# Moving the split weights by 16 bytes in the on-chip memory of a two-layer decoder trunk

## The chip, the cores and the metric

The kernel runs on one core of a Trainium2 chip. The metric is the device time of one execution in microseconds (us). Lower is better. The kernel before took 2561.69 us (median of three runs, 2560.36 to 2563.14).

## What is computed

The reference is a decoder trunk of two layers over 256 tokens of width 2048, all in float32. Layer 0 mixes the tokens by retention (8 heads), layer 1 by a short gated convolution. A SwiGLU feed-forward network (FFN) of inner width 5632 follows in each. Every sub-layer normalizes its input, scales and shifts it by values made from a conditioning vector, and multiplies its output by a gate made from the same vector.

```python
for i in range(DEPTH):                      # 2 layers
    mod = (silu(c) @ w_mod[i] + b_mod[i])   # six vectors of 2048
    sh1, sc1, g1, sh2, sc2, g2 = split(mod, 6)
    h = rms_norm(x, norm1_g[i]) * (1 + sc1) + sh1
    x = x + g1 * mixer(h)                   # layer 0: retention, layer 1: short convolution
    h = rms_norm(x, norm2_g[i]) * (1 + sc2) + sh2
    a, b = split(h @ ffn_w_in[i], 2)
    x = x + g2 * ((silu(a) * b) @ ffn_w_out[i])
return rms_norm(x, final_g)
```

## The kernel before

Nearly all the work is products of weights with 256 tokens. TensorE runs them in the type float32r, which carries fewer bits than float32. So each operand is split into a high part (the value rounded to float32r) and a low part (the rest), and three of the four partial products are summed: high times high, high times low, low times high.

**The way of a weight.** The weights lie in device memory in the order of their use, in 456 blocks of 128 x 2048 floats (1 MB). `fetch` (L378) loads a block into one of four `raw` tiles from SyncE's queue. `prepare` (L393) takes half a block, 1024 columns: ScalarE rounds it into `hi` (L419), VectorE subtracts that from the half and writes `lo` (L422). The tiles `hi` and `lo` have five places each (`PLACES`) of 1024 columns, used in turn. `take` (L434) hands the next columns of the place in front to TensorE and lets `prepare` run ahead.

**How a place is read.** A matmul has a stationary operand, 128 columns that are loaded into the array ahead of it, and a moving operand that streams through. The places are read in two ways:

- As the stationary operand. In `product` (L462) the 128 weight columns stand still and the activations move: 512 columns with `hi` (L472, high and low part of the 256 tokens at once), then 256 columns with `lo` (L475). `packed` (L497) does the same for narrow groups in three matmuls of 256 columns (L534 to L536), and `normed` (L644) at the start of a sub-layer with 258, 256 and 258 columns (L667 to L669). These carry the mixers' projections, the first columns of each FFN's input, and the output products of all but the last FFN.
- As the moving operand. In `by_token` (L492) and `sevens` (L1201) the activations of 128 tokens stand still and 512 weight columns move, in the three matmuls of `thrice` (L482): `hi` (L485), `lo` (L486), `hi` again with the activations' low part (L487). These carry most of the FFNs' input, the last FFN's output, and the values and gates of the retention. `sevens` forms a 2 x 2 block product from seven products instead of eight. Its sums of activations lie in tiles of their own (`sums`, `in_cb`, `u`, `sum`, `low`, `sums_of_tokens`).

The rest of the work shares VectorE and ScalarE with the splitting: the modulation vectors (VectorE, L326 and, at the start, L798), activations, gates and norms. The order of TensorE's instructions is written out by hand; the other engines are scheduled from priorities.

**Where the tiles lie.** A tile's pool gives it a start in each partition's memory; starts are rounded up to 32 bytes, and the tiles of a pool lie in the order in which they are first asked for. In the program before, `hi` starts at byte 43,616, `lo` at 64,096, the four `raw` at 84,576, 92,768, 100,960 and 109,152, an empty tile `aside` of 32 bytes at 117,344, and `h_all`, the activations, at 117,376. In steps of 64 bytes `hi`, `lo` and `raw` thus start at 32, `h_all` at 0. A place is 4096 bytes long and columns are taken 128 or 512 at a time, so every weight operand starts at 32 of 64. `rows_at(o)` (L628) lays 16 rows of 2048 bytes into `h_all`, from its start on (0 of 64) or from 120 floats on (`EARLIER`, 480 bytes, 32 of 64). The retention and both FFNs use the second, the convolution and the first columns of outputs the first. `normed` reads 16 rows (`raw_all`) of 514 floats, so row k starts at 8k bytes, modulo 128. The empty tiles `beside_cb`, `aside`, `beside`, `apart` and `beside_sums` do nothing but shift what lies behind them.

Of the kernel before, what the change touches and what calls it, by code (L numbers as in the profile page):

```python
# [10 lines left out]
F32 = mybir.dt.float32  # L11
F32R = mybir.dt.float32r
# [5 lines left out]
P = 128  # L18
# [14 lines left out]
HALF = 1024  # L33
# [18 lines left out]
STEPS = (8, 8, 24)  # L52
RAW_BUFS = 4
PLACES = 5
FETCHED, PLAIN, WARM, ADDED = 2, 3, (5, 0, 0, 0, 0, 0, 0, 8), ()
SIDE_BY_SIDE, HELD_SIDE_BY_SIDE = (5, 6, 7), (1, 3)
LEFT, ENDS, EARLIER = 8, 2, 120
# [207 lines left out]
def trunk(ctx: ExitStack, tc: tile.TileContext, x_in, c_in, pos_in, w_mod, cols_in, gain_in, tab_in, w_all, out):  # L265
# [3 lines left out]
    wpool = ctx.enter_context(tc.tile_pool(name="wpool", bufs=1))  # L269
# [123 lines left out]
    def prepare(between=None):  # L393
# [17 lines left out]
        elif piece == 5:  # L411
            nc.vector.tensor_tensor(b[3], b[3], b[1], op=ALU.subtract)
            raw = b[3]
        width, at = raw.shape[1], HALF * (taken_places[0] % PLACES)
        taken_places[0] += -(-width // HALF)
# [7 lines left out]
        ready.extend((hi[:, o], lo[:, o], o.stop - o.start) for o in steps)  # L423

    taken_places = [0]
    split_weights = [
        wpool.tile([P, PLACES * HALF], F32R, tag=tag, name=tag) for tag in ("hi", "lo")
    ]
    prepared = [0]

    def fits():
        return prepared[0] < len(pieces) and len(ready) + 1 + (pieces[prepared[0]][1] == 6) <= PLACES

# [184 lines left out]
    hpool = ctx.enter_context(tc.tile_pool(name="hpool", bufs=1))  # L618
# [2 lines left out]

    hpool.tile([P, LEFT], F32, tag="aside", name="aside")
    h_all = hpool.tile([P, (KT + 1) * (ENDS + 2 * S)], F32R, tag="h", name="h")
    hpool.tile([P, 88], F32, tag="beside", name="beside")

# [931 lines left out]
```

## Time and profile before

| what | value |
|---|---|
| median of three runs | 2561.69 us (2560.36 to 2563.14) |
| the profiled execution: span from the first to the last instruction | 2558.4 us |
| the median beside that span | 3.3 us more |
| granted TensorE clock, mean | 0.998 of full speed |
| VectorE busy | 2354.7 us (92%) |
| ScalarE busy | 1351.2 us (53%) |
| moved by DMA | 689.47 MB |

The profile is one execution seen by the hardware profiler; for it no time is given but its span. PE is TensorE's matmuls, PEld its loads of stationary operands, DVE is VectorE, ACT is ScalarE, POOL is GpSimd, SP is SyncE. In a row of a group, `bank<-hi,h` names what is written and what is read, `x1540` is the count, and the numbers behind the bar are the busy time in us, the mean duration of one in ns, and the idle time ahead of them. A matmul's duration in the profile holds the way through the array and overlaps the next one; what a matmul costs in a stream is the distance from its start to the start of the next, which the timeline shows to 10 ns.

### The profile page before, as it was taken

What the parts mean: (1) busy time and instruction counts of PE and PEld (TensorE: products, weight loads), DVE (VectorE), ACT (ScalarE), POOL (GpSimd) and SP (SyncE); (2) the same over time, 40 slices, a digit from 0 to 9 for tenths busy, and PEclk for the clock granted to TensorE, in tenths of its full rate; (3) what the DMA queues carried; (4) which work ended last, traced back from release to release, by engine and by line L of the source; (5) the groups of instructions that cost most, each with busy time, mean ns of one, the idle gap of its engine ahead of it and who ended that gap; (6) DMA issues with size and microseconds to landing.
All of it is one profiled execution on the core that took longest, in us unless ns stands there. A gap on an engine that the chain in (4) does not pass through costs nothing.

```text
span 2558.4 us, 34761 instructions
## 1 busy us (share of the span) xinstructions
PE 2539.3 (99%) x13237; PEld 2181.4 (85%) x13237; DVE 2354.7 (92%) x2968; ACT 1351.2 (53%) x1799; POOL 179.3 (7%) x234
## 2 busy tenths in 40 slices
PE   8999999999999999999999999999999999999998
PEld 7898888888889888888888898888998888888886
DVE  7989999898899999889999899888989999999998
ACT  5544543454456554345555454445566555555554
POOL 0000121011110001000000012000000000000001
PEclk9999999999999999999999999999999999999999
DMA  9987888879875667866667879888846465555653
GB/s 399 396 329 264 319 317 340 333 287 331 325 281 213 237 234 293 336 249 228 216 228 299 328 270 344 314 306 309 323 158 215 180 230 214 181 214 183 228 183 146
DMA packets 96695, 689.47 MB, mean 269 GB/s; under 512 B 10744, under 2 KB 12168, under 8 KB 13456
## 3 DMA queue, kind: packets, MB, share of 16 engines
q1 hardware_dynamic: 96528, 687.25, 72.2%
q8 instruction: 103, 1.69, 0.3%
q14 instruction: 64, 0.52, 0.1%
HBM read 685.11 MB, written 2.11 MB: 269 GB/s over the span
## 4 chain that ended last, share of the span: by engine, by line
PE 94%; DVE 3%; DMA 1%; ACT 1%; issue 1%; POOL 0%; SPq 0%; ACTq 0%; POOLq 0%; DVEq 0%
PE bank L472 22%; PE bank L487 17%; PE bank L485 17%; PE bank L486 17%; PE bank L475 11%; DVE lo L422 1%; PE bank L667 1%; PE bank L669 1%; PE bank L668 1%; PE bank L536 1%; PE bank L535 1%; PE bank L534 1%; DVE raw L798 1%; DMA raw<-w_all 1%; PE bank L1290 1%; PE bank L1067 1%
## 5 line engine op out<-in xcount | busy, mean ns | idle before, releaser
L419 ACT CAST hi<-raw 128x1024 fp32r<-128x1024 f32 (+1 forms) x984 | 991.1, 1019 | 936.7 <-PE bank L487 325.1
L422 DVE TENSOR_TENSOR lo<-raw,hi 128x1024 fp32r<-128x1024 f32 (+1 forms) x984 | 1143.3, 1179 | 125.6 <-ACT hi L419 116.7
L485 PE MATMUL bank<-hi,h 128*128 128x512 f32 x1540 | 602.9, 391 | 0.0
L487 PE MATMUL bank<-hi,h 128*128 128x512 f32 x1540 | 601.2, 390 | 0.0
L486 PE MATMUL bank<-lo,h 128*128 128x512 f32 x1540 | 601.1, 390 | 0.0
L326 DVE SCALAR_TENSOR_TENSOR raw<-raw,cb 128x2048 f32<-128x2048 f32 x160 | 365.4, 2285 | 8.2 <-DMA raw<-w_mod 8.0
L472 PE MATMUL bank<-h,hi 128*128 128x512 f32 x1012 | 352.8, 392 | 0.0
L487 PEld LDWEIGHTS bank<-hi,h 128*128 128x128 f32 x1540 | 289.4, 188 | 61.0
L485 PEld LDWEIGHTS bank<-hi,h 128*128 128x128 f32 x1540 | 289.6, 188 | 58.1
L486 PEld LDWEIGHTS bank<-lo,h 128*128 128x128 f32 x1540 | 289.7, 188 | 57.5
L472 PE MATMUL bank<-mid,hi 128*128 128x512 f32 x920 | 319.4, 391 | 0.0
L475 PE MATMUL bank<-h,lo 128*128 128x256 f32 x1012 | 285.0, 282 | 0.0
L475 PE MATMUL bank<-mid,lo 128*128 128x256 f32 x920 | 259.7, 282 | 0.0
L472 PEld LDWEIGHTS bank<-h,hi 128*128 128x128 f32 x1012 | 190.1, 188 | 40.3
L472 PEld LDWEIGHTS bank<-mid,hi 128*128 128x128 f32 x920 | 172.9, 188 | 35.6
L475 PEld LDWEIGHTS bank<-h,lo 128*128 128x128 f32 x1012 | 191.6, 189 | 0.5
L475 PEld LDWEIGHTS bank<-mid,lo 128*128 128x128 f32 x920 | 174.3, 189 | 0.1
L472 PE MATMUL bank<-rm,hi 128*128 128x512 f32 x496 | 172.5, 391 | 0.0
L475 PE MATMUL bank<-rm,lo 128*128 128x256 f32 x496 | 140.0, 282 | 0.0
L487 PE MATMUL bank<-hi,mid 128*128 128x512 f32 x284 | 110.9, 391 | 0.0
L485 PE MATMUL bank<-hi,mid 128*128 128x512 f32 x284 | 110.9, 391 | 0.0
L486 PE MATMUL bank<-lo,mid 128*128 128x512 f32 x284 | 110.7, 390 | 0.0
(300 smaller groups left out, 3344.2 us busy)
## 6 DMA issues: line engine op xcount, KB each, us to landing
raw<-w_all SPq DMA_DIRECT2D x456, 1024.0 KB, 5.0
raw<-w_mod SPq DMA_DIRECT2D x192, 1024.0 KB, 6.1
x<-x_in SPq DMA_DIRECT2D x4, 512.0 KB, 5.3
out<-xt SPq DMA_DIRECT2D x4, 512.0 KB, 3.0
decay<-tab_in SPq DMA_DIRECT2D x8, 128.0 KB, 4.9
x<-gate_row SPq DMA_DIRECT2D x2, 512.0 KB, 4.6
last_gain<-gain_in SPq DMA_DIRECT2D x1, 1024.0 KB
cols<-cols_in SPq DMA_DIRECT2D x1, 152.0 KB, 8.2
```

What stands on the lines that cost most here:

```text
L326: nc.vector.scalar_tensor_tensor(raw, raw, 1.0, cb, op0=ALU.mult, op1=ALU.mult, accum_out=total)
L419: nc.scalar.copy(hi[:, o], raw[:, o])
L422: nc.vector.tensor_tensor(lo, raw, hi.bitcast(F32), op=ALU.subtract)
L472: nc.tensor.matmul(pt, hi, h, start=fresh and k == g.ks[0], stop=False, skip_group_check=True)
L475: nc.tensor.matmul(pt[:, 1, :], lo, h[:, 0, :], start=False, stop=last and k == g.ks[-1], skip_group_check=True)
L485: nc.tensor.matmul(o, hi, w_hi, start=first, stop=False)
L486: nc.tensor.matmul(o, hi, w_lo, start=False, stop=False)
L487: nc.tensor.matmul(o, lo, w_hi, start=False, stop=last)
L534: nc.tensor.matmul(pt, hi, h[:, 0, :], start=first, stop=False, skip_group_check=True)
L535: nc.tensor.matmul(pt, hi, h[:, 1, :], start=False, stop=False, skip_group_check=True)
L536: nc.tensor.matmul(pt, lo, h[:, 0, :], start=False, stop=last, skip_group_check=True)
L667: nc.tensor.matmul(pt, hi, high, start=k == 0, stop=False, skip_group_check=True)
```

## The change

`hi` and `lo` are no longer two tiles but two stretches of one tile, which starts where `hi` started. The stretches begin four floats (`BEHIND`, 16 bytes) behind the tile's start. The tile has eight more floats (`LEFT`, 32 bytes) than the two tiles together, and the empty tile of eight floats ahead of `h_all` is gone.

```diff
+BEHIND = 4
 LEFT, ENDS, EARLIER = 8, 2, 120
...
-    split_weights = [
-        wpool.tile([P, PLACES * HALF], F32R, tag=tag, name=tag) for tag in ("hi", "lo")
-    ]
+    places = wpool.tile([P, 2 * PLACES * HALF + LEFT], F32R, tag="split", name="split")
+    split_weights = [places[:, o : o + PLACES * HALF] for o in (BEHIND, BEHIND + PLACES * HALF)]
...
-    hpool.tile([P, LEFT], F32, tag="aside", name="aside")
     h_all = hpool.tile([P, (KT + 1) * (ENDS + 2 * S)], F32R, tag="h", name="h")
```

By these sizes the places of `hi` start at byte 43,632 and those of `lo` at 64,112, both at 48 of 64. `h_all` stays at 117,376. The four `raw` tiles lie behind the places in the same pool, so by the sizes they start 32 bytes further on, at 84,608 and so on, 0 of 64. No instruction is added, removed or given another shape.

## The prediction

> **What bounds the kernel.** I read the profile's page first, then the waits of TensorE, then its groups by line, and last the timeline of single matmuls.
>
> ```profile
> span 2558.4 us, 34761 instructions
> ...
> PE 2539.3 (99%) x13237; PEld 2181.4 (85%) x13237; DVE 2354.7 (92%) x2968; ACT 1351.2 (53%) x1799; POOL 179.3 (7%) x234
> ...
> PE 94%; DVE 3%; DMA 1%; ACT 1%; issue 1%; POOL 0%; SPq 0%; ACTq 0%; POOLq 0%; DVEq 0%
> ```
>
> TensorE is busy for 99% of the span, and 94% of the chain of work that ended last runs through it. Its waits are small; the two largest are 3.5 us ahead of the first products and 1.8 us in three pieces:
>
> ```profile
> PE bank L593 <- POOL rs L925: 3.5, 1, 3.5
> PE bank L536 <- DVE lo L422: 1.8, 3, 0.9
> ```
>
> So the time is the number of matmuls times the distance from one start to the next. The change touches no count and no shape. It can move the time only if that distance depends on where an operand lies, or if a producer slows until TensorE waits for it. How many matmuls read a place, by line, over the whole span:
>
> ```profile
> 0.00:2560.00 2560.00, 804.61 (x2054) 386.19 (x2054) 1.00 0.72 269
> 0.00:2560.00 2560.00, 844.64 (x2428) 456.21 (x2428) 1.00 0.72 269
> 0.00:2560.00 2560.00, 89.56 (x316) 60.23 (x316) 1.00 0.72 269
> ```
>
> These are L485, L472 and L534. By the code L485 to L487 come in threes, L472 and L475 in twos, L534 to L536 in threes, and `normed` has three for each of 16 rows, 5 columns and 3 calls. That makes 6162 matmuls with weights as the moving operand, and 4856 + 948 + 720 = 6524 with weights as the stationary one: 12,686 of 13,237. The distances, from two quiet stretches of the timeline, 30 matmuls of L485 to L487 and 17 pairs of L472 and L475:
>
> ```profile
> 2298.17 0.39 PE L487 MATMUL bank<-hi,h 128*128 128x512 f32 x1
> ...
> 2304.97 0.39 PE L487 MATMUL bank<-hi,h 128*128 128x512 f32 x1
> ...
> 1600.01 0.39 PE L472 MATMUL bank<-h,hi 128*128 128x512 f32 x1
> ...
> 1605.90 0.39 PE L472 MATMUL bank<-h,hi 128*128 128x512 f32 x1
> ```
>
> 6.80 / 30 = 226.7 ns for a matmul of 512 columns, 5.89 / 17 = 346.5 ns for a pair of 512 and 256. In the first both operands start at 32 of 64 bytes. In the second the weights start at 32 and the activations at 0.
>
> **Part 1: the weights as moving and as stationary operand.** Does the place of an operand matter? Four groups of equal shape answer it:
>
> ```profile
> L485 PE MATMUL bank<-hi,sum 128*128 128x512 f32 x41 | 16.0, 390 | 0.0
> ...
> L485 PE MATMUL bank<-hi,sums 128*128 128x512 f32 x60 | 23.6, 394 | 0.0
> ...
> L534 PE MATMUL bank<-h,hi 128*128 128x256 f32 x260 | 73.9, 284 | 1.3 <-ACT h L826 1.3
> ...
> L534 PE MATMUL bank<-mid,hi 128*128 128x256 f32 x40 | 11.2, 279 | 0.0
> ```
>
> `sum` starts at 32 of 64 and `sums` at 0: with the stationary operand 32 bytes off the moving one, a matmul of 512 columns takes 4 ns more. In the other two the weights stand still at 32; with the moving `h` at 32 too it is 284 ns, with the moving `mid` at 0 it is 279 ns, 5 ns less. So the place counts, by some ns in 120 to 230, and not in one direction. The Trainium skill ("SBUF — State Buffer", section "Who interferes with whom") says that PE never waits on anyone for the memory, since its two read ports are its own. By that rule alone the sum would be 0 us, but the 390 against 394 ns say that place matters all the same.
>
> Shifts that are no multiple of 32 bytes are seen in one line group alone, `normed`, whose moving row k starts at 8k bytes (modulo 128) while its weights stand still at 32 of 64. A row k is 15 matmuls (five columns, three each; the middle one of the three starts 8 bytes further on). Its rows in the convolution's input, k = 0 and k = 10 to 15:
>
> ```profile
> 1488.93 0.28 PE L667 MATMUL bank<-h,hi 128*128 128x258 f32 x1
> ...
> 1490.72 0.28 PE L667 MATMUL bank<-h,hi 128*128 128x258 f32 x1
> ...
> 1508.13 0.28 PE L667 MATMUL bank<-h,hi 128*128 128x258 f32 x1
> ...
> 1509.94 0.29 PE L667 MATMUL bank<-h,hi 128*128 128x258 f32 x1
> ...
> 1511.74 0.28 PE L667 MATMUL bank<-h,hi 128*128 128x258 f32 x1
> ...
> 1513.54 0.28 PE L667 MATMUL bank<-h,hi 128*128 128x258 f32 x1
> ...
> 1515.32 0.28 PE L667 MATMUL bank<-h,hi 128*128 128x258 f32 x1
> ...
> 1517.12 0.28 PE L667 MATMUL bank<-h,hi 128*128 128x258 f32 x1
> ...
> 1518.89 0.39 PE L472 MATMUL bank<-h,hi 128*128 128x512 f32 x1
> ```
>
> That is 1.79 us for k = 0 (moving at 0 of 64), 1.81 for k = 10 (at 16), 1.80 for 11 (at 24), 1.80 for 12 (at 32), 1.78 for 13 (at 40), 1.80 for 14 (at 48) and 1.77 for 15 (at 56). I take what counts to be the stationary start less the moving one, modulo 64; this is a choice, since no row moves the weights themselves.
>
> - By-token matmuls, 6162: the difference goes from 0 to 32 - 48 = -16. Row 12 has 0, row 14 has -16: both 1.80 us, so 0 us.
> - Product pairs with activations at 0 of 64, 2104 pairs (all but the 324 of `h` in the retention and the FFNs' first columns): from 32 to 48, which is -16 again. Row 0 against row 14: 1.79 against 1.80 us, one step of the timeline's rounding, 0.7 ns a matmul at most, so 0 to +2.8 us for 4208 matmuls.
> - The other 324 pairs: from 0 to +16, row 12 against row 10: 1.80 against 1.81 us, 0.7 ns, +0.4 us for 648 matmuls.
> - The narrow groups (948) move by the same steps, at most 0.7 us; `normed` itself passes through all places before and after, so 0 us.
>
> The bounds: the fastest row shown, 1.77 us, is 2 ns a matmul below row 12, the slowest 0.7 ns above. Over 12,686 matmuls that is -25 to +8 us. If the 4 and 5 ns of the groups above applied to all, it would be +51 and -63 us; I use them below for one kind of reading at a time. I take the value by rows 12, 14 and 0, since they alone have a shift of 16 bytes: 0 to +4 us.
>
> The Trainium skill ("TensorE: Matmul & The Clock Gate", section "Back-to-back issue gap") gives N / 2.4 + 2.5 ns for an isolated matmul of N columns, an estimated 216 ns for 512. The trace's 226.7 ns is 11 ns above it, so by that formula a lucky place could give back some 11 ns a matmul; the rows above don't show it, and I give it no chance beyond the faster rival's.
>
> **Part 2: the producers.** ScalarE now writes `hi` at 48 and reads `raw` at 0 of 64, VectorE reads both and writes `lo` at 48; before, all lay at 32.
>
> ```profile
> L419 ACT CAST hi<-raw 128x1024 fp32r<-128x1024 f32 x906 | 946.3, 1053 | 899.5 <-PE bank L487 324.8 <-PE bank L472 291.4 <-DMA raw<-w_all 109.6
> ...
> L419 ACT CAST hi<-differences 128x1024 fp32r<-128x1024 f32 x30 | 31.6, 1053 | 33.7 <-PE bank L487 23.5 <-DVE differences L406 10.2
> ...
> L422 DVE TENSOR_TENSOR lo<-raw,hi 128x1024 fp32r<-128x1024 f32 x906 | 1096.0, 1221 | 124.8 <-ACT hi L419 115.9 <-PE bank L472 2.5
> ...
> L422 DVE TENSOR_TENSOR lo<-differences,hi 128x1024 fp32r<-128x1024 f32 x30 | 36.6, 1220 | 0.1
> ...
> 1520.00:1860.00 340.00, 340.00 (x2016) 304.22 (x2015) 306.95 (x420) 170.13 (x247) 35.08 (x49) 1.00 0.84 312
> ```
>
> `differences` lies at 0 of 64, `raw` at 32: 1053 and 1053 ns on ScalarE, 1221 and 1220 ns on VectorE. Place costs these engines nothing that shows; the bounds are -1 to +1 ns of one instruction. A start at 48 isn't among these rows. What hides it: in the densest stretch, 1520 to 1860 us, VectorE is busy for 306.95 of 340 us, ScalarE for 170.13. VectorE would have to slow by 10% before TensorE waited. If that cover were gone, each ns on L422 would cost about 1 us (906 long ones and some short). I count 0 us. The DMAs into `raw` land 32 bytes further on; ScalarE waits 109.6 us in all for them and TensorE not at all behind that, so 0 us, and no row tells the two places apart.
>
> The sum is 0 to +4 us on the span of 2558.4 us. The span lies 3.3 us under the median of the runs; with that added, and the lower half of the sum, I forecast 2562 us. About 0.2% (5.1 us) is what the measurement can tell from no change.
>
> **The rivals.**
>
> - *Faster: by-token streams run freer at 48.* For it speaks the 5 ns between `h` and `mid` as moving operands in L534: there the moving operand went from 32 to 0 (that is, 64), and 48 lies half way. Half of it, 2.5 ns, over 6162 matmuls is -15 us (2547 us), all of it -31 us (2531 us). Against it: rows 12 and 14 are equal.
> - *Slower: the weights stand worse at 48.* For it speak the 394 against 390 ns: a stationary operand that moved by 32 bytes cost 4 ns, and this one moves by 16. In the product pairs, 4856 matmuls, half of it is +10 us (2572 us) and all of it +19 us (2581 us). It decides the sign from 5.1 / 2428 = 2.1 ns a pair on. Against it: row 0 and row 14 are within the rounding.
> - *The change brings other than what it says.* With one tile for both stretches the scheduler could make ScalarE's next `hi` wait for VectorE's `lo`, and the `raw` tiles move too. One such wait per half block would put VectorE's 1.22 us behind ScalarE's 1.05, 2.27 us. A place lasts TensorE for 8 pairs of 346.5 or 12 matmuls of 226.7 ns, 2.7 us, which would hide it, but in `sevens` only for 6 matmuls, 1.36 us. There each of 3.5 places a block would cost 0.9 us; over the 30 blocks with `differences` (x30) alone that is +95 us (2657 us). Places within one tile are told apart already, so I think little of it.
>
> **How the numbers follow.** The forecast, place neutral within some us, has 0.41: of this 0.29 within 0.2%, and 0.06 on each side. The faster rival has 0.31, the slower one 0.25, the unintended wait 0.03, slower too. That gives 0.37 faster, 0.29 same, 0.34 slower. The forecast's own range is 2555 to 2568 us. For 8 in 10 it must reach to most of both rivals: from 2535 (most of the faster rival's full price) to 2586 us (the slower one's full price and 5 us more); the unintended wait stays outside.
>
> **What would show it.** If I am right, the changed kernel's timeline has 226 to 228 ns between by-token matmuls and 345 to 349 ns for a product pair, L419 and L422 stay within 10 ns, and TensorE's waits stay under 10 us. The faster rival shows as under 225 ns in L485 to L487 with the pairs unchanged, the slower one as pairs over 348.6 ns with L485 to L487 unchanged. New rows of TensorE waiting for L419 or L422 would show the unintended wait. I'm wrong if either distance has moved by over 1%, or if both kinds moved together: then the place itself counts and not the difference of the two operands.

## The result and the profile after

The changed kernel takes 2586.85 us (median of four runs, 2586.43 to 2588.31), beside 2561.2 us (2560.36 to 2563.14) for the kernel before. The ratio is 1.0100, with a 95% interval from 1.0086 to 1.0114: one per cent slower. The profiled span is 2584.7 us, 26.3 us longer than before.

The starts that the program allots are as the change says: the common tile at byte 43,616, so the places at 48 of 64 bytes, `raw` from 84,608 on (0 of 64), `h_all` at 117,376 as before. TensorE's granted clock is 0.999 of full speed, beside 0.998, so the clock has no part in the loss. In the changed kernel `hi` and `lo` both carry the name `split`, ScalarE's rounding is L420 and VectorE's subtraction L423. L472 to L536 have kept their numbers.

From the page of the changed kernel: the span, the engines' busy time, the shares of the chain.

```profile
span 2584.7 us, 34761 instructions
...
PE 2564.7 (99%) x13237; PEld 2177.0 (84%) x13237; DVE 2355.8 (91%) x2968; ACT 1352.7 (52%) x1799; POOL 175.5 (7%) x234
...
PE 96%; DVE 2%; DMA 1%; ACT 1%; issue 0%; POOL 0%; ACTq 0%; POOLq 0%; SPq 0%; DVEq 0%
```

TensorE's busy time has grown by 25.4 us, that of VectorE and ScalarE by 1.1 and 1.5. The two largest waits of TensorE in the changed kernel (total, times, longest):

```profile
PE bank L593 <- POOL rs L924: 3.5, 1, 3.5
PE bank L536 <- DVE split L423: 2.1, 4, 0.9
```

The others are 1.5 us and less, as before. So TensorE waits for nothing of weight that it did not wait for before. Its own matmuls stand further apart. Where along the run this happens can be read from the starts of a few matmuls in both timelines (start in us, duration). First the kernel before:

```profile
201.76 0.40 PE L485 MATMUL bank<-hi,h 128*128 128x512 f32 x1
...
366.36 0.47 PE L472 MATMUL bank<-rm,hi 128*128 128x512 f32 x1
...
438.55 0.39 PE L472 MATMUL bank<-h,hi 128*128 128x512 f32 x1
...
994.47 0.48 PE L472 MATMUL bank<-mid,hi 128*128 128x512 f32 x1
...
1099.94 0.39 PE L485 MATMUL bank<-hi,h 128*128 128x512 f32 x1
...
1361.19 0.48 PE L472 MATMUL bank<-mid,hi 128*128 128x512 f32 x1
...
1896.40 0.40 PE L485 MATMUL bank<-hi,h 128*128 128x512 f32 x1
...
2548.49 0.39 PE L487 MATMUL bank<-hi,mid 128*128 128x512 f32 x1
```

Then the same matmuls in the changed kernel:

```profile
201.60 0.40 PE L485 MATMUL bank<-split,h 128*128 128x512 f32 x1
...
367.89 0.47 PE L472 MATMUL bank<-rm,split 128*128 128x512 f32 x1
...
441.44 0.39 PE L472 MATMUL bank<-h,split 128*128 128x512 f32 x1
...
1004.17 0.48 PE L472 MATMUL bank<-mid,split 128*128 128x512 f32 x1
...
1109.65 0.39 PE L485 MATMUL bank<-split,h 128*128 128x512 f32 x1
...
1374.90 0.48 PE L472 MATMUL bank<-mid,split 128*128 128x512 f32 x1
...
1910.47 0.40 PE L485 MATMUL bank<-split,h 128*128 128x512 f32 x1
...
2575.11 0.39 PE L487 MATMUL bank<-split,mid 128*128 128x512 f32 x1
```

The changed kernel lags by -0.16, 1.53, 2.89, 9.70, 9.71, 13.71, 14.07 and 26.62 us at these eight points. Read the differences between neighbours:

- From 994 to 1100 us, 304 product pairs of `mid`, it loses 0.01 us. From 1361 to 1896 us, which is `normed` and product pairs of `mid` and `h`, it loses 0.36 us.
- From 1100 to 1361 us, nearly all by-token matmuls, it loses 4.00 us. From 1896 us to the end, by-token too, it loses 12.55 us.
- From 366 to 439 us, 208 product pairs of `rm` (the retention's output), it loses 1.36 us, 6.5 ns a pair.

The whole sum needs all matmuls. I took from each trace the distance from a matmul's start to TensorE's next start. Distances of 260 ns and more (180 ns and more in the narrow groups and `normed`) are left out; they are breaks between stretches.

| kind | count | before, ns | after, ns | count x difference, us |
|---|---|---|---|---|
| by-token matmul (L485 to L487) | 6162 | 227.71 | 231.66 | +24.3 |
| product pair, `rm` moving | 496 | 346.79 | 352.78 | +3.0 |
| product pair, `mid` moving | 920 | 346.72 | 346.88 | +0.1 |
| product pair, `h` moving from 0 of 64 | 688 | 346.67 | 346.67 | 0.0 |
| product pair, `h` moving from 32 of 64 | 324 | 349.26 | 346.98 | -0.7 |
| narrow groups (L534 to L536) | 948 | 118.92 | 117.93 | -0.9 |
| `normed` | 720 | 119.26 | 119.69 | +0.3 |

The sum is +26.1 us, and the span grew by 26.3. The loss is 4 ns on each by-token matmul. A quiet stretch of them in the changed kernel:

```profile
2298.07 0.40 PE L485 MATMUL bank<-split,sum 128*128 128x512 f32 x1
...
2298.76 0.40 PE L485 MATMUL bank<-split,h 128*128 128x512 f32 x1
2298.99 0.40 PE L486 MATMUL bank<-split,h 128*128 128x512 f32 x1
2299.23 0.39 PE L487 MATMUL bank<-split,h 128*128 128x512 f32 x1
2299.46 0.39 PE L485 MATMUL bank<-split,h 128*128 128x512 f32 x1
2299.68 0.40 PE L486 MATMUL bank<-split,h 128*128 128x512 f32 x1
...
2305.02 0.39 PE L485 MATMUL bank<-split,h 128*128 128x512 f32 x1
```

Thirty matmuls take 6.95 us, 231.7 ns each, where 30 took 6.80 us before. The distances are not all alike: 0.23, 0.24, 0.23, 0.22 us, and so on. In the trace's nanoseconds the steady stream repeats four distances, 235, 230, 228 and 234, whatever line they are from. Before, it went 227, 227, 226. So the stream has fallen into another rhythm, and no single line has become dear.

Finally the groups that the prediction had read before, in the changed kernel (count, busy us, mean ns, idle time ahead):

```profile
L485 PE MATMUL bank<-split,sums 128*128 128x512 f32 x60 | 23.6, 393 | 0.0
L485 PE MATMUL bank<-split,sum 128*128 128x512 f32 x41 | 16.2, 395 | 0.0
...
L534 PE MATMUL bank<-h,split 128*128 128x256 f32 x260 | 73.6, 283 | 1.5 <-ACT h L825 1.5
...
L420 ACT CAST split<-raw 128x1024 fp32r<-128x1024 f32 x906 | 947.2, 1053 | 915.9 <-PE bank L487 351.4 <-PE bank L472 304.8 <-DMA raw<-w_all 94.9
...
L423 DVE TENSOR_TENSOR split<-raw,split 128x1024 fp32r<-128x1024 f32 x906 | 1094.5, 1219 | 131.4 <-ACT split L420 127.1
```

The 4 ns by which `sum` had stood below `sums` are gone: it is now 395 against 393. ScalarE and VectorE take what they took, 1053 and 1219 ns.

### The profile page after: what moved, and what is told of

It is laid out like the page before. It is cut to its first block, busy times and chain, and to the rows that moved or that the text cites. A ratio compares the mean times of both kernels' runs of the same rounds, so it can differ in the third digit from the quotient of the medians.

```text
span 2584.7 us, 34761 instructions
## 1 busy us (share of the span) xinstructions
PE 2564.7 (99%) x13237; PEld 2177.0 (84%) x13237; DVE 2355.8 (91%) x2968; ACT 1352.7 (52%) x1799; POOL 175.5 (7%) x234
## 4 chain that ended last, share of the span: by engine, by line
PE 96%; DVE 2%; DMA 1%; ACT 1%; issue 0%; POOL 0%; ACTq 0%; POOLq 0%; SPq 0%; DVEq 0%
PE bank L472 22%; PE bank L485 18%; PE bank L486 18%; PE bank L487 18%; PE bank L475 11%; PE bank L666 1%; PE bank L667 1%; PE bank L668 1%; PE bank L536 1%; PE bank L535 1%; PE bank L534 1%; DVE raw L797 1%; PE bank L1289 1%; DMA raw<-w_all 1%; PE bank L1066 1%; DMA raw<-w_mod 1%
## 5 line engine op out<-in xcount | busy, mean ns | idle before, releaser
L420 ACT CAST split<-raw 128x1024 fp32r<-128x1024 f32 (+1 forms) x984 | 992.1, 1019 | 952.7 <-PE bank L487 352.1
L423 DVE TENSOR_TENSOR split<-raw,split 128x1024 fp32r<-128x1024 f32 (+1 forms) x984 | 1141.8, 1177 | 132.2 <-ACT split L420 127.9
L485 PE MATMUL bank<-split,h 128*128 128x512 f32 x1540 | 608.5, 395 | 0.0
L486 PE MATMUL bank<-split,h 128*128 128x512 f32 x1540 | 606.8, 394 | 0.0
L487 PE MATMUL bank<-split,h 128*128 128x512 f32 x1540 | 606.6, 394 | 0.0
L472 PE MATMUL bank<-h,split 128*128 128x512 f32 x1012 | 352.1, 392 | 0.0
L487 PEld LDWEIGHTS bank<-split,h 128*128 128x128 f32 x1540 | 289.6, 188 | 67.3
L485 PEld LDWEIGHTS bank<-split,h 128*128 128x128 f32 x1540 | 289.6, 188 | 63.9
L486 PEld LDWEIGHTS bank<-split,h 128*128 128x128 f32 x1540 | 289.7, 188 | 63.4
L472 PE MATMUL bank<-mid,split 128*128 128x512 f32 x920 | 319.5, 392 | 0.0
L475 PE MATMUL bank<-h,split 128*128 128x256 f32 x1012 | 283.0, 280 | 0.0
L475 PE MATMUL bank<-mid,split 128*128 128x256 f32 x920 | 256.8, 279 | 0.0
L472 PEld LDWEIGHTS bank<-h,split 128*128 128x128 f32 x1012 | 190.1, 188 | 41.5
L472 PEld LDWEIGHTS bank<-mid,split 128*128 128x128 f32 x920 | 173.0, 188 | 38.2
L475 PEld LDWEIGHTS bank<-h,split 128*128 128x128 f32 x1012 | 190.2, 188 | 0.5
L472 PE MATMUL bank<-rm,split 128*128 128x512 f32 x496 | 175.5, 396 | 0.0
L475 PEld LDWEIGHTS bank<-mid,split 128*128 128x128 f32 x920 | 172.7, 188 | 0.1
L472 PEld LDWEIGHTS bank<-rm,split 128*128 128x128 f32 x496 | 93.7, 189 | 21.9
L485 PE MATMUL bank<-split,mid 128*128 128x512 f32 x284 | 112.0, 394 | 0.0
L486 PE MATMUL bank<-split,mid 128*128 128x512 f32 x284 | 111.9, 394 | 0.0
```

The costliest lines, as they stand in the source:

```text
L420: nc.scalar.copy(hi[:, o], raw[:, o])
L423: nc.vector.tensor_tensor(lo, raw, hi.bitcast(F32), op=ALU.subtract)
L472: nc.tensor.matmul(pt, hi, h, start=fresh and k == g.ks[0], stop=False, skip_group_check=True)
L475: nc.tensor.matmul(pt[:, 1, :], lo, h[:, 0, :], start=False, stop=last and k == g.ks[-1], skip_group_check=True)
L485: nc.tensor.matmul(o, hi, w_hi, start=first, stop=False)
L486: nc.tensor.matmul(o, hi, w_lo, start=False, stop=False)
```

## The experiments

The theory after the result: the start of the weights, as TensorE's moving operand, decides the rhythm of the by-token stream by itself. Its rivals: the difference between the starts of the two operands decides (the prediction's choice); the move of `raw` or the common tile does it; the writes of ScalarE and VectorE to the places disturb TensorE's reads.

All edits are to the changed kernel. "183 matmuls" below is one uninterrupted by-token stretch in the last FFN. Its first and last start, in the kernel before and then in the changed one:

```profile
2264.95 0.47 PE L485 MATMUL bank<-hi,h 128*128 128x512 f32 x1
...
2306.33 0.39 PE L487 MATMUL bank<-hi,h 128*128 128x512 f32 x1
```

```profile
2286.17 0.48 PE L485 MATMUL bank<-split,h 128*128 128x512 f32 x1
...
2328.41 0.39 PE L487 MATMUL bank<-split,h 128*128 128x512 f32 x1
```

That is 41.38 / 182 = 227.4 ns before and 42.24 / 182 = 232.1 ns in the changed kernel.

**e1, the raw tiles alone.** The places are one tile still, but begin at its start, at 32 of 64 again. `raw` stays at 0 of 64.

```diff
-BEHIND = 4
+BEHIND = 0
```

> The places go back to 32 of 64 bytes, as before, but stay in one tile, and the raw tiles stay 32 bytes further on (0 of 64). If the raw tiles' move or the one tile costs the time, this run keeps the change's time, about 2587 us, and by-token matmuls stay at about 231.7 ns. If the start of the moving operand costs it, or its difference to the stationary one, the time is that of before, 2561 us within 5 us, and by-token matmuls are at 227 ns again.

2560.53 us, ratio 0.9998 (0.9989 to 1.0007), by-token 227.7 ns, pairs 347.1 ns. The 183 matmuls take 41.38 us again:

```profile
2265.36 0.47 PE L485 MATMUL bank<-split,h 128*128 128x512 f32 x1
...
2306.74 0.39 PE L487 MATMUL bank<-split,h 128*128 128x512 f32 x1
```

The common tile and the new place of `raw` cost nothing. All of the loss comes from the 16 bytes.

**e2, the places at 0 of 64.**

```diff
-BEHIND = 4
+BEHIND = 8
```

> The places start 32 bytes further on than before, at 0 of 64. If what costs is a moving operand that starts at an odd multiple of 16 bytes, by-token matmuls are at about 227 ns and the time is near 2561 us. If it is the difference between the stationary and the moving start, which is 32 here, by-token matmuls take what those with a stationary operand 32 off took before, about 231 ns, and the time is about 2585 us.

2602.88 us, ratio 1.0163 (1.0148 to 1.0178): by-token 233.0 ns, pairs 351.3 ns. Neither of the two readings gives this time: going 16 bytes further costs more still. Here the product pairs of `mid` and `h` lose too, which they did not in the changed kernel. One part of the by-token stream does better. The 250 matmuls whose stationary operand (`sums`, `in_cb`) lies at 0 as well take 229.8 ns, the others 233.2; in the kernel before it was the other way round, 231.6 and 227.5. So where the two operands lie to each other has some part.

**e3, the activations moved along.** The rows of `h` lie 16 bytes further on as well, so that the difference between the operands is again what it was.

```diff
-            h_all[:, o + 2 * S * j : ...
+            h_all[:, BEHIND + o + 2 * S * j : ...
```

> As the change, and the rows of h start 16 bytes further on as well, so that in 4620 of 6162 by-token matmuls the stationary and the moving operand again start at the same place of 64 bytes (48). If the difference counts, these go back to about 227 ns and some 20 us come back, to about 2567 us. If the moving operand's own start counts, by-token matmuls stay at about 231.7 ns and the time at about 2587 us.

2587.16 us, ratio 1.0102 (1.0087 to 1.0117). The 183 matmuls, with weights and `h` at 48:

```profile
2286.95 0.47 PE L485 MATMUL bank<-split,h 128*128 128x512 f32 x1
...
2329.14 0.39 PE L487 MATMUL bank<-split,h 128*128 128x512 f32 x1
```

42.19 / 182 = 231.8 ns with a difference of zero, as slow as in the changed kernel. So the difference of the starts within 64 bytes isn't what decides. This is where the prediction's choice falls.

**e4, only `lo` moved.** `hi` begins at 32 of 64, `lo` at 48.

```diff
-... for o in (BEHIND, BEHIND + PLACES * HALF)]
+... for o in (0, BEHIND + PLACES * HALF)]
```

> Only the places of lo start 16 bytes further on; those of hi are back at 32 of 64. If the moving operand's own start counts, L486 alone (moving lo) is slow, at about 232 ns, L485 and L487 (moving hi) are at about 227 ns, and a third of the loss stays, to about 2569 us. If it were the whole stream that falls into another rhythm, all three lines would slow together by less or more than that third.

2586.83 us, ratio 1.0098 (1.0082 to 1.0115): the whole loss, though of the three by-token lines only L486 reads a place that has moved. The 183 matmuls:

```profile
2286.22 0.48 PE L485 MATMUL bank<-split,h 128*128 128x512 f32 x1
...
2328.52 0.39 PE L487 MATMUL bank<-split,h 128*128 128x512 f32 x1
```

42.30 / 182 = 232.4 ns. Over all by-token matmuls the distances are 230.8 ns (L485), 231.8 (L486) and 233.4 (L487). The two lines that read `hi` at 32 have slowed as well. One stream in three slows all, and into a rhythm of its own: in nanoseconds it repeats after fifteen distances, from 224 to 241. The product pairs stay at 346.9 ns, with `rm` at 347.5.

**e5, without the splitting.** The roundings and subtractions run for the first ten half blocks only, and after that TensorE reads what lies in the places; the line numbers of the products are one higher.

```diff
-        for o in steps:
-            nc.scalar.copy(hi[:, o], raw[:, o])
+        if taken_places[0] <= 2 * PLACES:
+            for o in steps:
+                nc.scalar.copy(hi[:, o], raw[:, o])
...
-        nc.vector.tensor_tensor(lo, raw, hi.bitcast(F32), op=ALU.subtract)
+            nc.vector.tensor_tensor(lo, raw, hi.bitcast(F32), op=ALU.subtract)
```

> As the change (places at 48 of 64 bytes), but only the first ten half blocks are rounded and subtracted into the places; after that TensorE reads what lies there, so L420 and L423 write nothing more and the output isn't the reference's. If TensorE's own two operands set the by-token rhythm, its matmuls stay at about 231.7 ns. If the writes of ScalarE and VectorE into the places at 48 disturb its reads, they go back to about 227 ns.

2583.82 us in one run. The engines on the page of this kernel, and then the 183 matmuls in its timeline:

```profile
PE 2564.0 (99%) x13237; PEld 2176.9 (84%) x13237; DVE 1235.5 (48%) x1916; ACT 325.2 (13%) x747; POOL 99.6 (4%) x234
```

```profile
2283.72 0.48 PE L486 MATMUL bank<-split,h 128*128 128x512 f32 x1
...
2325.96 0.39 PE L488 MATMUL bank<-split,h 128*128 128x512 f32 x1
```

ScalarE's busy share has gone from 52% to 13% and VectorE's from 91% to 48%, yet the stretch takes 42.24 us to the hundredth as in the changed kernel, with the same four distances. The writes to the places have no part in it. The loads into `raw` still run here, and e1 shows only that their place costs nothing. That the rhythm arises between TensorE's own accesses is what is left, argued and not shown.

**e6, e8, e10: other starts.** `BEHIND` is 2, 6 and 12 floats. For the last one the tile is 16 floats longer and the empty tile `beside` 16 shorter, which moves `h` by 64 bytes.

```diff
-BEHIND = 4
+BEHIND = 2      (e6; 6 in e8, 12 in e10)
```

> The places start 8 bytes further on than before, at 40 of 64. If only starts at a multiple of 32 bytes run at 226.7 ns, by-token matmuls take 230 ns or more and the time is 2580 us or more. By the rows of normed, where a moving row 8 bytes past the weights was 1.78 against 1.80 us, they would be about 1 ns faster than before and the time about 2553 us.

> The places start 24 bytes further on than before, at 56 of 64. The same two readings as for 8 bytes: 230 ns or more and 2580 us or more if only multiples of 32 bytes run at 226.7 ns; by the rows of normed (1.77 us for the row 24 bytes past the weights, against 1.80) some 2 ns faster than before, about 2549 us.

> The same as the run with 64 bytes, but the stretches begin 48 bytes behind the tile's start, so every place starts at 16 of 64. If 32 of 64 is the one good start for the moving weights: 2585 to 2608 us, by-token matmuls at 231 to 234 ns. If the start within 32 bytes decides (16 as 48): 2587 us within 4 us. If only starts in the upper half of the 64 bytes are slow: 2561 us, 227 ns, which the run with 0 of 64 speaks against.

2600.69 us (ratio 1.0157, 1.0142 to 1.0172), 2607.52 us (1.0184, 1.0167 to 1.0201) and 2603.91 us (1.0164, 1.0147 to 1.0181). All three are slower than the change, and of the starts tried only 32 gives the fast rhythm. The table after e9 has them together.

**e7, only `h` moved.** The places are at 32 of 64 as before, the rows of `h` 16 bytes further on.

```diff
-BEHIND = 4
+BEHIND = 0
...
-            h_all[:, o + 2 * S * j : ...
+            h_all[:, 4 + o + 2 * S * j : ...
```

> The places are back at 32 of 64, and the rows of h alone start 16 bytes further on, so in 4620 by-token matmuls the stationary operand is at 48 and the moving one at 32. If the moving operand alone sets the rhythm, the time is that of before, 2561 us. If any difference of the two by 16 bytes costs, whichever is moved, by-token matmuls with h take about 231 ns and the time is about 2580 us.

2571.25 us, ratio 1.0041 (1.0026 to 1.0056). Two stretches of 183 by-token matmuls in this kernel's timeline:

```profile
916.53 0.48 PE L485 MATMUL bank<-split,u 128*128 128x512 f32 x1
...
958.72 0.40 PE L487 MATMUL bank<-split,h 128*128 128x512 f32 x1
...
2274.40 0.48 PE L485 MATMUL bank<-split,h 128*128 128x512 f32 x1
...
2315.98 0.39 PE L487 MATMUL bank<-split,h 128*128 128x512 f32 x1
```

The first has 42.19 / 182 = 231.8 ns, the second 228.5, and the time lies between the two readings. In nanoseconds each stretch holds pieces of 227, 227, 226 and pieces of a slow rhythm of 233, 235, 234, 233, 233, 232. In the second, the fast rhythm sets in at matmuls with `sum` (32 of 64) and then holds for every `h` behind them. In the first, it breaks off where `sums` (0 of 64) comes. Of the 4620 by-token matmuls with `h`, 2465 have a distance of 226 or 227 ns. So with the moving weights at 32 and the stationary `h` at 48 both rhythms occur, with the same starts. The stationary operand's place has a say too, but a lesser one: 229.7 ns on average with `h`, against 227.6 before. So the theory has to be widened: the place of each operand counts, the moving one most, and so, it seems, does the rhythm that the stream is already in.

**e9, 64 bytes further on.** Places at 32 of 64 again, but 64 bytes from where they were. `h` moves by 64 bytes too.

```diff
-BEHIND = 4
+BEHIND = 16
...
-    places = wpool.tile([P, 2 * PLACES * HALF + LEFT], ...
+    places = wpool.tile([P, 2 * PLACES * HALF + LEFT + 16], ...
...
-hpool.tile([P, 88], F32, tag="beside", name="beside")
+hpool.tile([P, 72], F32, tag="beside", name="beside")
```

> The stretches begin 64 bytes behind the tile's start instead of 16, so that every place starts at 32 of 64 again, but 64 bytes away from where it was before; h starts 64 bytes further on too (0 of 64, as before). If only the start within 64 bytes counts: 2561 us within 4 us, 226 to 229 ns between the starts of by-token matmuls. If the absolute place counts, or the distance from the tile's start, or a longer period than 64 bytes: 2570 to 2605 us, with by-token matmuls at 230 to 234 ns.

2572.06 us, ratio 1.0043 (1.0029 to 1.0058): neither of the two expectations as a whole. The 183 matmuls of this kernel, after two stretches of `rm` pairs (416 and 384 matmuls):

```profile
203.42 0.40 PE L485 MATMUL bank<-split,h 128*128 128x512 f32 x1
...
368.35 0.47 PE L472 MATMUL bank<-rm,split 128*128 128x512 f32 x1
...
440.42 0.28 PE L475 MATMUL bank<-rm,split 128*128 128x256 f32 x1
...
702.45 0.48 PE L472 MATMUL bank<-rm,split 128*128 128x512 f32 x1
...
770.25 0.28 PE L475 MATMUL bank<-rm,split 128*128 128x256 f32 x1
...
2275.80 0.48 PE L485 MATMUL bank<-split,h 128*128 128x512 f32 x1
...
2317.22 0.39 PE L487 MATMUL bank<-split,h 128*128 128x512 f32 x1
```

This by-token stretch is back in the fast rhythm: 41.42 / 182 = 227.6 ns, and 228.0 ns over all 6162. But only the matmuls with `h`, which moved along by 64 bytes, are where they were (227.4 ns, 227.6 before). Those whose stationary operand lies at 32 of 64 too but stayed in its place, `mid` and `u` among them, went from 227.3 to 229.3 ns. The pairs are alike: those of `h` from 0 of 64, moved along, stay at 346.7 ns, and those of `mid` and `rm`, which stayed, lose. The first `rm` stretch has 72.07 / 415 = 173.7 ns a matmul, 347 ns a pair, and the second 67.80 / 383 = 177.0, 354 ns a pair, with the same shapes and the same starts within 64 bytes. Pairs of `mid` take 353.1 ns on average. So a product stretch falls into a rhythm, in this run one of two, and keeps it, and what chooses isn't the start within 64 bytes alone. That most of what moved along kept its time and what stayed lost some points to the distance between the two operands over more than 64 bytes. No run moves that alone, and the pairs of `h` from 32 of 64 lost 1.6 ns though they moved along, so it is not shown. By kind the pairs cost 920 x 6.4 + 496 x 3.1 + 324 x 1.6 ns = 7.9 us, the by-token matmuls 1.8 us; the first by-token matmul starts 1.7 us later than before (203.42 against 201.76). That makes 11.4 of the 11.8 us by which this span (2570.2 us) is longer.

The starts together, with `mid` and `rm` where they were, and `h` too but for e9 and e10, where it lies 64 bytes further on:

| places start at, of 64 | run | time, us | by-token, ns | product pair, ns |
|---|---|---|---|---|
| 0 | e2 | 2602.88 | 233.0 | 351.3 |
| 16 | e10 | 2603.91 | 234.4 | 348.0 |
| 32 | before | 2561.2 | 227.7 | 347.1 |
| 32, 64 bytes on | e9 | 2572.06 | 228.0 | 350.3 |
| 40 | e6 | 2600.69 | 233.2 | 350.4 |
| 48 | the change | 2586.85 | 231.7 | 348.0 |
| 56 | e8 | 2607.52 | 233.6 | 351.1 |

Why 32 gives the fast by-token rhythm stays open, and so does what puts a product stretch into one rhythm or another. No version tried beats the kernel before.

## Why the prediction was wrong, point by point

- *What bounds the kernel.* Right. TensorE is busy for 99% of the span and waits for nothing new, so the time moved with the distances between its matmuls.
- *The place counts, by some ns and not in one direction.* Right: 0 to 6.7 ns on a by-token matmul in the table above.
- *"I take what counts to be the stationary start less the moving one, modulo 64."* This is the step that failed, and with it the by-token term of 0 us. In e3 the difference was kept and the stream was as slow as in the changed kernel. The term measured 6162 x 3.95 ns = +24.3 us, nearly the whole loss. How the operands lie to each other has a part of its own (e2), but not by this rule.
- *The rows it was read from.* `normed` moves activations of 256 and 258 columns, and its rows at the various starts differ by 2.7 ns a matmul at most. There a start at 56 was the cheapest, 2 ns below 32, while by-token weights at 56 cost 5.9 ns more than at 32. These rows carried over neither in size nor in sign to 512 moving weight columns. The prediction had a nearer row, `sum` against `sums` in L485 itself, with the right shape and the right lines. Its 4 ns (a difference of durations; from start to start it is 5 ns, 226.6 against 231.6), which the prediction noted as +51 us if they applied to all and then set aside, are about what each by-token matmul lost. That the size agrees is no proof of one cause. It does show that the bounds of -25 to +8 us were too narrow, since they came from `normed` alone.
- *Product pairs, 0 to +2.8 us and +0.4 us.* The sizes were near (+3.1 and -0.7 us), by luck, since the kind was wrong: `rm` lost 6 ns a pair while `mid` and `h` lost nothing, and the pairs of `h` from 32 of 64 became 2.3 ns shorter. It is a rhythm held through a stretch, and no price of a place on every pair.
- *The narrow groups and `normed`, at most 0.7 and 0 us.* Measured -0.9 and +0.3 us.
- *The producers and the raw tiles, 0 us.* Right: 1053 and 1219 ns, and e1 is within 0.1% of the kernel before.
- *The rivals.* The slower one had the sign and, at 2581 us, nearly the size, but sought the loss in the product pairs, so that its size came near by luck. The faster one named the stream that did move, with the wrong sign; the 5 ns that spoke for it are durations, and from start to start the same groups (L534 to L536) differ by 2.8 ns, 119.4 against 116.7. The unintended wait does not occur.
- *What would show it.* "I'm wrong if either distance has moved by over 1%": the by-token distance moved by 1.7%, from 227.71 to 231.66 ns, while most pairs stayed.

The Trainium skill ("SBUF — State Buffer", section "Who interferes with whom") says that no other engine's access holds TensorE up. The runs agree: e5 took ScalarE from 52% to 13% and VectorE from 91% to 48% and left the by-token distance at 231.7 ns. Beside that the runs show that the place of TensorE's own operands is worth 4 to 7 ns on a by-token matmul. The Trainium skill's formula for the spacing of isolated matmuls ("TensorE: Matmul & The Clock Gate", section "Back-to-back issue gap") gives an estimated 216 ns for 512 columns. The steady streams here went 226.7 ns at best, and no start that was tried came nearer to it.

## What to carry to other kernels

Where a kernel is a dense stream of matmuls, as this one is, the start of each operand in its partition is a parameter like any other: print the starts, vary them in steps of 8 or 16 bytes, and look at the distances from start to start, since the waits don't show the effect. A row that shows an operand's place on one shape or in one role says little about another; price such a change by the nearest row in the same lines, and keep both signs open. Shift a tile only with the starts of all tiles behind it in view.

## What the runs showed that was not expected

- A stream of float32r matmuls settles into a rhythm of a few distances and keeps it over hundreds of matmuls. By token it is 227, 227, 226 ns in the kernel before and 235, 230, 228, 234 ns in the changed one. For product pairs it is 347 or 353 ns there, with other values between in e6, e7 and e8. In e7 the same matmuls with the same starts run in two rhythms; what ran ahead of them seems to choose.
- One stream in three can slow all three: with only `lo` at 48, the lines that read `hi` at 32 slowed too, from 227.9 to 230.8 ns (L485) and from 227.7 to 233.4 ns (L487).
- Sixty-four bytes brought the by-token rhythm back where `h` moved along (227.4 ns), not quite with the operands that stayed (229.3 ns), and put the pairs of `mid` into a slower one (353.1 against 346.7 ns). So the start within 64 bytes doesn't tell the whole.
